# A chunked scan beside attention: the scan's steps divided anew

## The chip, the core and the metric

The kernel runs on one core of a Trainium2 chip. The metric is the device time in microseconds of one execution. The engines named below are TensorE (PE; its weight loads are PEld), VectorE (DVE), ScalarE (ACT), GpSimd (POOL) and SyncE (SP), whose queue issues most of the DMA transfers. All values are float32. A product marked 128*128 uses the whole array of TensorE, one marked 64*64 a quarter of it.

## The reference

One layer of a hybrid encoder for 1024 prompt tokens and 32 sample tokens that share the weights. `proj = x @ w_in` is split among three mixers: latent attention with 6 heads, a diagonal state space model (S5), and RWKV-7 time mixing with 6 heads of 64. Their outputs are concatenated, go through `w_out`, a layer norm, a squared-ReLU MLP of width 4096 and a second layer norm. The change lies in RWKV-7, whose recurrence for one head is

```python
def step(S, inp):
    r_t, w_t, k_t, v_t, kk_t, a_t = inp
    sa = jnp.einsum('bhij,bhj->bhi', S, -kk_t)
    S = (S * w_t[:, :, None, :] + sa[..., None] * (kk_t * a_t)[:, :, None, :]
         + v_t[..., None] * k_t[:, :, None, :])
    return S, jnp.einsum('bhij,bhj->bhi', S, r_t)
```

followed by a normalization of each head's output, a bonus term, a gate, and the final state as an output.

## The kernel before

The kernel has four parts in time: the input projections; attention and the scan side by side; the output projection with its layer norm; the MLP with the last layer norm.

The scan works on blocks of 128 tokens (two chunks of 64), nine of them in `ORDER` = (8, 0, 1, ..., 7), where block 8 holds the 32 sample tokens. Within a chunk the recurrence becomes products of 64 x 64 matrices, one for each of the 6 heads and 2 chunks. Heads go in three pairs: the two heads of a pair stand on partitions 0 to 63 and 64 to 127. So each product uses one quarter of TensorE's array, and which quarter follows from where its operands and its output lie. In `stage_rwkv` (L999) the pass i of the loop works on three blocks at once: t = ORDER[i] gets its chunk products and its solve, u = ORDER[i-1] gets its operators, its state steps and its mean, v = ORDER[i-2] is normalized and stored. The parts, with the names of their PSUM tiles:

- `rwkv_pairs` (t): pra, products masked by causality (L833, L835 on DVE); prt, four transposes for each of three head pairs (L840, copied by ACT in L841); prb (L846, L848); the weights of the bonus on POOL (L853, L854) and their sum prk (L856, L858).
- `rwkv_norm` (v): prv (L985), the inverse root on DVE and ACT, two POOL operations (L993, L994), a store to mg_d.
- `rwkv_ops` (u): prg, the transition and the readout (L897; L899 and L900 on DVE); pru, the sums U and Y (L906 to L912), a step for each head pair; then L917 (DVE) and L919 (ACT).
- `rwkv_nv` (t): prn (L868, L869). `rwkv_chain` (u): for each chunk pry (readout from the state, L940), prs (the new state, L944), L946 and L947 on DVE. `rwkv_mean` (u): prm (L968). `rwkv_solve` (t): prw with the inverse of the chunk's triangular matrix (L882, L883).

All of these tiles come from one PSUM pool, `g.pr`, with three slots; a tile waits until a slot has been released by its last reader.

What sets the order: all parts are generators, and each `yield` ends a step. `side_by_side` (L1299) takes steps from attention (with S5 among them) and from the scan in turn. After each scan step it lets RATIO attention steps pass (10 and 14 at the start). Every step's TensorE instructions are queued behind the last one of the step before (`issue_after`), so TensorE's order is the order of steps; within a step, and on the other engines, a scheduler orders at compile time by priority and estimated times, with the scan's steps 120 places ahead:

```python
while (n >= 1 or done[1]) and not done[0]:
    step(0, a)
    n -= 1
if not done[1]:
    ...
        step(1, b)
k += 1
n += LEAD[k] if k < len(LEAD) else RATIO
```

Every engine works through its own queue in order. When both streams are done, the output projection follows: `out_early` and `out_mm` for the first three token tiles, whose products the scheduler may place as soon as their operands are there, then `out_tile` (L1466) for the others, which loads its part of mg_d by L1431 and the residual z by L1478 in SP's queue. `out_weights` loads the eight tiles of `w_out` (L55, split in L49 and L50) into memory that the scan has given up: three at the end of pass 8, five after the loop.

Of the kernel before, what the change touches and what calls it, by code (L numbers as in the profile page):

```python
# [712 lines left out]
def hsl(i):  # L713
    return slice(64 * i, 64 * i + 64)
# [104 lines left out]
K_A, K_B, K_K, K_V, K_NV, K_N, K_KR, K_BR = range(8)  # L819


def rwkv_pairs(g, t):

    nc = g.nc
    mm = nc.tensor.matmul
    ld = g.ld[t]
    r = g.rp.tile([P, 3, 8, 2, 64], F32, tag="r", name="r", bufs=2)
    g.r[t] = r

    pa = [g.pr.tile([P, 3, 2, 64], F32, tag="pr", name="pra") for _ in range(2)]  # L830
    for p in range(3):
        for h, c in DIAG:
            mm(out=pa[h][hsl(c), p], lhsT=ld[hsl(h), p, 2, hsl(c)], rhs=ld[hsl(h), p, 0:5:4, hsl(c)], start=True, stop=True)  # L833
# [3 lines left out]
    for p in range(3):  # L837
        pt = g.pr.tile([P, 4, P], F32, tag="pr", name="prt")
        for i in range(4):
            nc.tensor.transpose(out=pt[:, i], in_=ld[:, p, i], identity=g.ident)  # L840
        nc.scalar.activation(out=r[:, p, 0:4].rearrange("q a h x -> q a (h x)"), in_=pt, func=AF.Copy)  # L841
        yield
    pb = [g.pr.tile([P, 3, 64], F32, tag="pr", name="prb") for _ in range(2)]
    for p in range(3):
        for h, c in DIAG:
            mm(out=pb[h][hsl(c), p], lhsT=ld[hsl(h), p, 1, hsl(c)], rhs=ld[hsl(h), p, 4, hsl(c)], start=True, stop=True)  # L846
    for h in range(2):
        nc.vector.tensor_tensor(out=r[:, :, K_BR, h], in0=pb[h], in1=bc(g.msk[:, 1:2], [P, 3, 64]), op=ALU.mult)  # L848
    yield

    w = blk_tokens(t)[1]
    x = r[:, :, K_NV].rearrange("q p h x -> q p (h x)")[:, :, :w]
    nc.gpsimd.tensor_tensor(out=x, in0=ld[:, :, 2, :w], in1=ld[:, :, 4, :w], op=ALU.mult)  # L853
    nc.gpsimd.tensor_tensor(out=x, in0=x, in1=bc(g.vec[:, V_RK:V_RK + 3][:, :, None], [P, 3, w]), op=ALU.mult)  # L854
    ps = g.pr.tile([P, 3, P], F32, tag="pr", name="prk")[:, :, :w]
    mm(out=ps, lhsT=g.bones, rhs=x, start=True, stop=True)  # L856
    g.bn[t] = g.rl.tile([P, 3, P], F32, tag="bn", name="bn", bufs=3)[:, :, :w]
    nc.vector.tensor_tensor(out=g.bn[t], in0=ps, in1=ld[:, :, 3, :w], op=ALU.mult)  # L858


def rwkv_nv(g, t):
# [7 lines left out]
    nc.scalar.activation(out=r[:, :, K_NV], in_=pn, func=AF.Copy)  # L869


def rwkv_solve(g, t):
    nc = g.nc
    r = g.r[t]
    wu = g.rp.tile([P, 3, 2, 2, 64], F32, tag="wu", name="wu", bufs=1)
    g.wu[t] = wu
    for p0, p1 in ((0, 2), (2, 3)):
        pw = g.pr.tile([P, p1 - p0, 2, 2, 64], F32, tag="pr", name="prw")
        for p in range(p0, p1):
            for h in range(2):  # L880
                for c in range(2):
                    nc.tensor.matmul(out=pw[hsl(c), p - p0, h], lhsT=g.xt[p][hsl(c), t, h], rhs=r[hsl(c), p, K_A:K_NV + 1:K_NV, h], start=True, stop=True)  # L882
        nc.scalar.activation(out=wu[:, p0:p1], in_=pw, func=AF.Copy)  # L883


def rwkv_ops(g, t):

    nc = g.nc
    mm = nc.tensor.matmul
    r, wu, ld = g.r.pop(t), g.wu.pop(t), g.ld.pop(t)  # L890
    gq = g.rl.tile([P, 2, 3, 3, 64], F32, tag="gq", name="gq", bufs=1)
    g.gq[t] = gq
    nch = 2 if t < 8 else 1
    pg = [g.pr.tile([P, 3, 2, 64], F32, tag="pr", name="prg") for _ in range(2)]
    for p in range(3):
        for c, h in DIAG:
            mm(out=pg[c][hsl(h), p], lhsT=wu[hsl(c), p, h, 0], rhs=r[hsl(c), p, K_B:K_BR + 1:K_BR - K_B, h], start=True, stop=True)  # L897
    for c in range(nch):
        nc.vector.tensor_tensor(out=gq[:, c, 0], in0=pg[c][:, :, 0], in1=bc(g.i2[:, None], [P, 3, 64]), op=ALU.add)  # L899
        nc.vector.tensor_tensor(out=gq[:, c, 1], in0=pg[c][:, :, 1], in1=ld[:, :, 4, hsl(c)], op=ALU.add)  # L900
    yield
    pu = [g.pr.tile([P, 3, 2, 64], F32, tag="pr", name="pru") for _ in range(2)]
    for p in range(3):
        for hc in (DIAG[0:2], DIAG[2:4]):
            for c, h in hc:
                mm(out=pu[c][hsl(h), p, 0], lhsT=r[hsl(c), p, K_B, h], rhs=wu[hsl(c), p, h, 1], start=True, stop=False)  # L906
            for c, h in hc:
                mm(out=pu[c][hsl(h), p, 0], lhsT=r[hsl(c), p, K_K, h], rhs=r[hsl(c), p, K_V, h], start=False, stop=True)
            for c, h in hc:
                mm(out=pu[c][hsl(h), p, 1], lhsT=wu[hsl(c), p, h, 1], rhs=r[hsl(c), p, K_BR, h], start=True, stop=False)  # L910
            for c, h in hc:
                mm(out=pu[c][hsl(h), p, 1], lhsT=r[hsl(c), p, K_V, h], rhs=r[hsl(c), p, K_KR, h], start=False, stop=True)  # L912
        yield
    yb = g.yb[t]
    for c in range(nch):
        k = 2 * t + c
        nc.vector.tensor_tensor(out=gq[:, c, 2], in0=pu[c][:, :, 0], in1=bc(g.pc[:, :, k:k + 1], [P, 3, 64]), op=ALU.mult)  # L917
        w = min(64, blk_tokens(t)[1])
        nc.scalar.activation(out=yb[:, :, 64 * c:64 * c + w], in_=pu[c][:, :, 1, :w], func=AF.Copy)  # L919


def rwkv_chain(g, t):

    nc = g.nc
    mm = nc.tensor.matmul
    gq = g.gq.pop(t)
    nch = 2 if t < 8 else 1
    py = g.pr.tile([P, 3, 2, 64], F32, tag="pr", name="pry")
    for c in range(nch):
        k = 2 * t + c  # L930
        if k in (0, 16):
            g.st = g.rl.tile([P, 3, 64], F32, tag="st", name="st", bufs=3)
            if k == 0:
                nc.gpsimd.memset(g.st, 0.0)
            else:
                nc.sync.dma_start(out=g.st, in_=g.a["s0"].rearrange("p j i -> j p i"))
        st = g.st
        for p in range(3):
            for h in range(2):
                mm(out=py[hsl(h), p, c], lhsT=st[hsl(h), p], rhs=gq[hsl(h), c, 1, p], start=True, stop=True)  # L940
        ps = g.pr.tile([P, 3, 64], F32, tag="pr", name="prs")
        for p in range(3):
            for h in range(2):
                mm(out=ps[hsl(h), p], lhsT=gq[hsl(h), c, 0, p], rhs=st[hsl(h), p], start=True, stop=True)  # L944
        sn = g.rl.tile([P, 3, 64], F32, tag="st", name="st", bufs=3)
        nc.vector.tensor_tensor(out=sn, in0=ps, in1=bc(g.pc[:, :, k:k + 1], [P, 3, 64]), op=ALU.mult)  # L946
        nc.vector.tensor_tensor(out=sn, in0=sn, in1=gq[:, c, 2], op=ALU.add)  # L947
        g.st = sn
        yield
        if k >= 15:  # L950
            pt = g.pr.tile([P, 3, P], F32, tag="pr", name="prq")
            for p in range(3):
                nc.tensor.transpose(out=pt[0:64, p], in_=sn[:, p], identity=g.ident)
            so = g.rl.tile([P, 3, P], F32, tag="m", name="so", bufs=1)[0:64]
            nc.scalar.activation(out=so, in_=pt[0:64], func=AF.Copy)
            nc.scalar.dma_start(out=g.o["rw_p" if k == 15 else "rw_s"].rearrange("h i j -> i h j"), in_=so.rearrange("i p (h j) -> i (p h) j", h=2))
    w = blk_tokens(t)[1]
    ys = g.yb[t][:, :, :w]
    nc.vector.tensor_tensor(out=ys, in0=ys, in1=py[:, :, 0:nch].rearrange("q p c x -> q p (c x)")[:, :, :w], op=ALU.add)


def rwkv_mean(g, t):
# [36 lines left out]
def stage_rwkv(g):  # L999
# [9 lines left out]
    for p in range(3):  # L1009
# [7 lines left out]
            nc.sync.dma_start(out=x[0:32, 0:16, 32:64], in_=src[c][2][:, 0:16])  # L1017
        g.xt[p] = xt

    for i in range(10):  # L1020
        t, u, v = (ORDER[j] if 0 <= j < 9 else None for j in (i, i - 1, i - 2))
        if i + 2 < 9:
            rwkv_load(g, ORDER[i + 2])
        if t is not None:
            yield from rwkv_pairs(g, t)
        if v is not None:
            rwkv_norm(g, v)
            yield
        if u is not None:
            g.yb[u] = g.rl.tile([P, 3, P], F32, tag="yb", name="yb", bufs=2)  # L1030
            yield from rwkv_ops(g, u)
        if t is not None:
            rwkv_nv(g, t)
            yield
            if u is not None:
                yield from rwkv_chain(g, u)
                rwkv_mean(g, u)
            rwkv_solve(g, t)
            yield
        if i == 8:  # L1040
            out_weights(g, WOUT[:3])
    out_weights(g, WOUT[3:])


def stage_rwkv_end(g):
    yield from rwkv_chain(g, ORDER[8])
    rwkv_mean(g, ORDER[8])
    rwkv_norm(g, ORDER[8])


# [10 lines left out]
    yield from stage_rwkv_end(g)  # L1061


RATIO, LEAD, PRIO = 2.5, (10, 14), 120
S5_FROM, S5_STEP = 50, 7


# [803 lines left out]
```

## Time and profile before

| | us |
|---|---|
| median of 3 runs | 1610.53 (1609.14 to 1616.11) |
| the profiled execution | 1609.9 |
| its span, first to last instruction | 1608.1 |
| TensorE busy | 1487.7 (93%) |
| VectorE busy | 920.6 (57%) |
| ScalarE busy | 510.6 (32%) |
| GpSimd busy | 415.9 (26%) |

The first product of the scan's first block (pra) starts at 366.24 us, the last products of attention (av) at 722.69, the last of the scan (prv) at 744.77. In the rows, a timeline line has start, length, engine, line of the code, operation, output<-inputs, shape and count; in brackets stands how long the engine was idle before and what ended that.

### The profile page before, as it was taken

How to read it: one execution, taken by the hardware profiler on the slowest of the kernel's cores; microseconds unless marked ns; L12 is line 12 of the kernel's file. 1: busy time of each engine (PE TensorE's matmuls, PEld its weight loads, DVE VectorE, ACT ScalarE, POOL GpSimd, SP SyncE). 2: the span in 40 equal slices, each digit the busy share in tenths (PEclk: the TensorE clock that was granted, in tenths of full speed). 3: DMA queues.
4: the chain of work that ended last, by engine and by line, in shares of the span. 5: the costliest groups of instructions: out<-in, count | busy, mean ns of one | idle time of the engine just before them, and what ended most of it. 6: DMA issues, size and time to landing. Idle time of an engine off the chain costs nothing. (4 is left out here: it accounts for less than half of the span.)

```text
span 1608.1 us, 26358 instructions
## 1 busy us (share of the span) xinstructions
PE 1487.7 (93%) x10855; PEld 1336.1 (83%) x10855; DVE 920.6 (57%) x1676; ACT 510.6 (32%) x991; POOL 415.9 (26%) x394
## 2 busy tenths in 40 slices
PE   7899898578899798888999999999999999999995
PEld 7889786466667566566879999999999999999995
DVE  8476959363566544453865755554454454545457
ACT  5344433314544545542323212222121112221122
POOL 4623663511121101211422221222121112221123
PEclk9999999788999999999999999999999999999998
DMA  5314471437233221233512111111111111111012
GB/s 183 132 59 175 148 191 31 115 87 127 71 86 87 63 75 42 72 98 92 174 56 79 40 40 41 52 53 49 44 43 50 40 40 53 53 40 53 14 41 82
DMA packets 112621, 123.50 MB, mean 77 GB/s; under 512 B 51280, under 2 KB 87812, under 8 KB 112120
## 3 DMA queue, kind: packets, MB, share of 16 engines
q1 hardware_dynamic: 92516, 102.53, 21.8%
q10 hardware_dynamic: 19632, 18.27, 3.8%
q8 instruction: 85, 1.39, 0.4%
q0 software_dynamic: 352, 1.01, 0.2%
q14 instruction: 36, 0.29, 0.1%
HBM read 89.05 MB, written 32.68 MB: 76 GB/s over the span
## 5 line engine op out<-in xcount | busy, mean ns | idle before, releaser
L63 PE MATMUL acc<-xh,uphi 128*128 128x384 f32 (+1 forms) x768 | 249.0, 324 | 0.0
L65 PE MATMUL acc<-xl,uphi 128*128 128x384 f32 (+1 forms) x768 | 248.1, 323 | 0.0
L67 PE MATMUL acc<-xh,uplo 128*128 128x384 f32 (+1 forms) x768 | 247.8, 323 | 0.0
L1538 DVE TENSOR_TENSOR rl<-rl 128x384 f32<-128x384 f32 (+1 forms) x96 | 142.2, 1481 | 176.2 <-ACT rl L1537 174.3
L1566 DVE TENSOR_TENSOR yacc<-yacc,acc 128x384 f32<-128x384 f32 (+2 forms) x344 | 158.9, 508 | 112.1 <-PE acc L67 112.0
L63 PE MATMUL acc<-hh,dnhi 128*128 128x384 f32 (+2 forms) x736 | 209.3, 320 | 0.0
L65 PE MATMUL acc<-hl,dnhi 128*128 128x384 f32 (+2 forms) x736 | 207.2, 320 | 0.0
L67 PE MATMUL acc<-hh,dnlo 128*128 128x384 f32 (+2 forms) x736 | 197.5, 319 | 0.0
L50 POOL TENSOR_TENSOR dnlo<-dnraw,dnhi 128x1024 fp32r<-128x1024 f32 x30 | 72.5, 2417 | 336.8 <-ACT dnhi L49 321.5
L63 PEld LDWEIGHTS acc<-xh,uphi 128*128 128x128 f32 x768 | 144.2, 188 | 0.2 <-ACT xh L49 0.2
L65 PEld LDWEIGHTS acc<-xl,uphi 128*128 128x128 f32 x768 | 144.3, 188 | 0.0
L67 PEld LDWEIGHTS acc<-xh,uplo 128*128 128x128 f32 x768 | 144.3, 188 | 0.0
L50 POOL TENSOR_TENSOR uplo<-upraw,uphi 128x1024 fp32r<-128x1024 f32 x34 | 81.6, 2401 | 238.3 <-ACT uphi L49 238.3
L63 PE MATMUL acc<-xh,wmhi 128*128 128x384 f32 (+3 forms) x384 | 131.9, 344 | 9.3 <-ACT xh L49 8.2
L65 PE MATMUL acc<-xl,wmhi 128*128 128x384 f32 (+3 forms) x384 | 130.2, 339 | 1.6 <-DVE xl L50 1.6
L63 PEld LDWEIGHTS acc<-hh,dnhi 128*128 128x128 f32 x736 | 131.6, 188 | 0.0
L65 PEld LDWEIGHTS acc<-hl,dnhi 128*128 128x128 f32 x736 | 131.5, 188 | 0.0
L67 PE MATMUL acc<-xh,wmlo 128*128 128x384 f32 (+3 forms) x384 | 129.6, 338 | 0.0
L67 PEld LDWEIGHTS acc<-hh,dnlo 128*128 128x128 f32 x736 | 128.9, 188 | 0.0
L49 ACT ACTIVATE dnhi<-dnraw 128x1024 fp32r<-128x1024 f32 x30 | 31.8, 1060 | 298.9 <-PE acc L65 249.2
L49 ACT ACTIVATE hh<-rl 128x384 fp32r<-128x384 f32 (+1 forms) x96 | 47.9, 499 | 148.7 <-DVE rl L1538 148.7
L63 PEld LDWEIGHTS acc<-xh,wmhi 128*128 128x128 f32 (+1 forms) x384 | 73.9, 192 | 12.8 <-ACT xh L49 8.5
(489 smaller groups left out, 2881.2 us busy)
## 6 DMA issues: line engine op xcount, KB each, us to landing
upraw<-in_w_up SPq DMA_DIRECT2D x32, 512.0 KB
dnraw<-in_w_dn SPq DMA_DIRECT2D x30, 512.0 KB
ld<-rw SPq DMA_DIRECT2D x24, 320.0 KB
wmraw<-in_w_m SPq DMA_DIRECT2D x12, 512.0 KB
wo<-in_w_out SPq DMA_DIRECT2D x8, 512.0 KB
z<-in_xa SPq DMA_DIRECT2D x8, 512.0 KB
out_y<-o SPq DMA_DIRECT2D x8, 512.0 KB
xr<-in_xt SPq DMA_DIRECT2D x8, 384.0 KB
```

Of the source, the lines that this page charges most:

```text
L49: nc.scalar.activation(out=hi, in_=ps, func=AF.Copy)
L50: (lo_eng or nc.vector).tensor_tensor(out=lo, in0=ps, in1=hi.bitcast(F32), op=ALU.subtract)
L63: nc.tensor.matmul(out=outs[i], lhsT=lh, rhs=rhs[i][0], start=start, stop=False)
L65: nc.tensor.matmul(out=outs[i], lhsT=lh, rhs=rhs[i][1], start=False, stop=False)
L67: nc.tensor.matmul(out=outs[i], lhsT=ll, rhs=rhs[i][0], start=False, stop=stop)
L1538: nc.vector.tensor_tensor(out=r[:, :n], in0=r[:, :n], in1=r[:, :n], op=ALU.mult)
L1566: nc.vector.tensor_tensor(out=y, in0=y, in1=ps[i][:, :n], op=ALU.add)
```

## The change

The arithmetic stays the same. The scan's functions are cut so that each can be called by itself, and the loop puts them into other steps. `rwkv_pairs` becomes `rwkv_causal`, `rwkv_turn` (one head pair), `rwkv_br`, `rwkv_weigh` (the POOL part of the bonus) and `rwkv_bonus`; `rwkv_ops` becomes `rwkv_gq` and `rwkv_uy`; `rwkv_solve` takes a range of head pairs; `rwkv_chain` does one chunk, with the products for the new state ahead of those for the readout; the transposes of the final states are `rwkv_state`. A full pass has 9 steps instead of 14:

| before | after |
|---|---|
| pra | pra |
| prt of pair 0 | prt of pairs 0 and 1 |
| prt of pair 1 | weights of the bonus, prt of pair 2, prm of v |
| prt of pair 2 | prb |
| prb | prk, normalization of v |
| prk, normalization of v | prg, prn |
| prg | pru of all three pairs, U and Y evicted |
| pru of pair 0 | state step of chunk 0, prw of pairs 0 and 1 |
| pru of pair 1 | state step of chunk 1, prw of pair 2 |
| pru of pair 2 | |
| U and Y evicted, prn | |
| state step of chunk 0 | |
| state step of chunk 1 | |
| end of the chain, prm of u, prw | |

The mean of a block (prm) so moves from its own pass into the next. The last block's state steps move into the loop, ahead of the loads of the last five output weights. RATIO goes from 2.5 to 3.6.

```diff
     for i in range(10):
         t, u, v = (ORDER[j] if 0 <= j < 9 else None for j in (i, i - 1, i - 2))
         if i + 2 < 9:
             rwkv_load(g, ORDER[i + 2])
         if t is not None:
-            yield from rwkv_pairs(g, t)
+            rwkv_causal(g, t)
+            yield
+            rwkv_turn(g, t, 0)
+            rwkv_turn(g, t, 1)
+            yield
+            x = rwkv_weigh(g, t)
+            rwkv_turn(g, t, 2)
+        if v is not None:
+            rwkv_mean(g, v)
+            if v == 8:
+                rwkv_state(g, 16)
+        yield
+        if t is not None:
+            rwkv_br(g, t)
+            yield
+            rwkv_bonus(g, t, x)
         if v is not None:
             rwkv_norm(g, v)
-            yield
+        yield
         if u is not None:
             g.yb[u] = g.rl.tile([P, 3, P], F32, tag="yb", name="yb", bufs=2)
-            yield from rwkv_ops(g, u)
+            rwkv_gq(g, u)
         if t is not None:
             rwkv_nv(g, t)
+        yield
+        if u is not None:
+            rwkv_uy(g, u)
             yield
-            if u is not None:
-                yield from rwkv_chain(g, u)
-                rwkv_mean(g, u)
-            rwkv_solve(g, t)
-            yield
+            rwkv_chain(g, u, 0)
+        if t is not None:
+            rwkv_solve(g, t, 0, 2)
+        yield
+        if u is not None and chunks(u) > 1:
+            rwkv_chain(g, u, 1)
+        if t is not None:
+            rwkv_solve(g, t, 2, 3)
+        yield
         if i == 8:
             out_weights(g, WOUT[:3])
     out_weights(g, WOUT[3:])
...
 def stage_rwkv_end(g):
-    yield from rwkv_chain(g, ORDER[8])
     rwkv_mean(g, ORDER[8])
+    rwkv_state(g, 15)
+    yield
     rwkv_norm(g, ORDER[8])
...
-def rwkv_chain(g, t):
+def rwkv_chain(g, t, c):
...
+    gq = g.gq[t]
+    if c == 0:
+        g.py = g.pr.tile([P, 3, 2, 64], F32, tag="pr", name="pry")
+    k = 2 * t + c
...
+    st = g.st
+    ps = g.pr.tile([P, 3, 64], F32, tag="pr", name="prs")
+    for p in range(3):
+        for h in range(2):
+            mm(out=ps[hsl(h), p], lhsT=gq[hsl(h), c, 0, p], rhs=st[hsl(h), p], start=True, stop=True)
+    for p in range(3):
+        for h in range(2):
+            mm(out=g.py[hsl(h), p, c], lhsT=st[hsl(h), p], rhs=gq[hsl(h), c, 1, p], start=True, stop=True)
...
-def rwkv_ops(g, t):
+def rwkv_uy(g, t):
...
     pu = [g.pr.tile([P, 3, 2, 64], F32, tag="pr", name="pru") for _ in range(2)]
     for p in range(3):
         for hc in (DIAG[0:2], DIAG[2:4]):
...
-        yield
...
-RATIO, LEAD, PRIO = 2.5, (10, 14), 120
+RATIO, LEAD, PRIO = 3.6, (10, 14), 120
```

More of the change, by code (lines that the diff above doesn't have):

```diff
@@ L819, with rwkv_causal @@
 K_A, K_B, K_K, K_V, K_NV, K_N, K_KR, K_BR = range(8)
[L822 removed]
+def rwkv_causal(g, t):
     nc = g.nc
[L825 removed]
     ld = g.ld[t]
@@ L869, in rwkv_nv, with rwkv_solve, chunks, rwkv_gq @@
     nc.scalar.activation(out=r[:, :, K_NV], in_=pn, func=AF.Copy)
-def rwkv_solve(g, t):
+def rwkv_solve(g, t, p0, p1):
     nc = g.nc
     r = g.r[t]
[L875 to L883, printed above, removed]
-def rwkv_ops(g, t):
+    if p0 == 0:
+        g.wu[t] = g.rp.tile([P, 3, 2, 2, 64], F32, tag="wu", name="wu", bufs=1)
+    pw = g.pr.tile([P, p1 - p0, 2, 2, 64], F32, tag="pr", name="prw")
+    for p in range(p0, p1):
+        for h in range(2):
+            for c in range(2):
+                nc.tensor.matmul(out=pw[hsl(c), p - p0, h], lhsT=g.xt[p][hsl(c), t, h], rhs=r[hsl(c), p, K_A:K_NV + 1:K_NV, h], start=True, stop=True)
+    nc.scalar.activation(out=g.wu[t][:, p0:p1], in_=pw, func=AF.Copy)
+def chunks(t):
+    return 2 if t < 8 else 1
+def rwkv_gq(g, t):
     nc = g.nc
-    mm = nc.tensor.matmul
-    r, wu, ld = g.r.pop(t), g.wu.pop(t), g.ld.pop(t)
+    r, wu, ld = g.r[t], g.wu[t], g.ld.pop(t)
     gq = g.rl.tile([P, 2, 3, 3, 64], F32, tag="gq", name="gq", bufs=1)
     g.gq[t] = gq
-    nch = 2 if t < 8 else 1
     pg = [g.pr.tile([P, 3, 2, 64], F32, tag="pr", name="prg") for _ in range(2)]
@@ L912, in rwkv_ops @@
                 mm(out=pu[c][hsl(h), p, 1], lhsT=r[hsl(c), p, K_V, h], rhs=r[hsl(c), p, K_KR, h], start=False, stop=True)
-        yield
     yb = g.yb[t]
-    for c in range(nch):
+    for c in range(chunks(t)):
         k = 2 * t + c
@@ L919, in rwkv_ops @@
         nc.scalar.activation(out=yb[:, :, 64 * c:64 * c + w], in_=pu[c][:, :, 1, :w], func=AF.Copy)
-def rwkv_chain(g, t):
+def rwkv_chain(g, t, c):
     nc = g.nc
     mm = nc.tensor.matmul
[L926 to L959, printed above, removed]
@@ new lines, in rwkv_chain @@
+    for p in range(3):
+        for h in range(2):
+            mm(out=g.py[hsl(h), p, c], lhsT=st[hsl(h), p], rhs=gq[hsl(h), c, 1, p], start=True, stop=True)
+    sn = g.rl.tile([P, 3, 64], F32, tag="st", name="st", bufs=3)
+    nc.vector.tensor_tensor(out=sn, in0=ps, in1=bc(g.pc[:, :, k:k + 1], [P, 3, 64]), op=ALU.mult)
+    nc.vector.tensor_tensor(out=sn, in0=sn, in1=gq[:, c, 2], op=ALU.add)
+    g.st = sn
+    if c == chunks(t) - 1:
+        w = blk_tokens(t)[1]
+        ys = g.yb[t][:, :, :w]
+        nc.vector.tensor_tensor(out=ys, in0=ys, in1=g.py[:, :, 0:c + 1].rearrange("q p c x -> q p (c x)")[:, :, :w], op=ALU.add)
+        g.gq.pop(t)
@@ L962, in rwkv_mean, with rwkv_state @@
+def rwkv_state(g, k):
+    nc = g.nc
+    pt = g.pr.tile([P, 3, P], F32, tag="pr", name="prq")
+    for p in range(3):
+        nc.tensor.transpose(out=pt[0:64, p], in_=g.st[:, p], identity=g.ident)
+    so = g.rl.tile([P, 3, P], F32, tag="m", name="so", bufs=1)[0:64]
+    nc.scalar.activation(out=so, in_=pt[0:64], func=AF.Copy)
+    nc.scalar.dma_start(out=g.o["rw_p" if k == 15 else "rw_s"].rearrange("h i j -> i h j"), in_=so.rearrange("i p (h j) -> i (p h) j", h=2))
 def rwkv_mean(g, t):
```

54 lines of the change are left out of this document (36 added, 18 removed).

## The prediction

> **What bounds the kernel now.** I read the engine shares and the 40 slices first, then busy time by stage, then who waits for whom on TensorE in the stage that the change touches, and last the order of instructions there. The chain of waits on the page covers only the last few instructions, so it is not used.
>
> ```profile
> PE 1487.7 (93%) x10855; PEld 1336.1 (83%) x10855; DVE 920.6 (57%) x1676; ACT 510.6 (32%) x991; POOL 415.9 (26%) x394
> PE   7899898578899798888999999999999999999995
> ```
>
> TensorE is busy 93% of the span, and from slice 20 on it is full: what is gained before about 780 us is kept to the end. The stages (stretch, length, busy us of PE, PEld, DVE, ACT, POOL, then granted clock and DMA):
>
> ```profile
> 366.00:706.00 340.00, 303.86 (x3207) 225.08 (x3207) 180.96 (x408) 166.97 (x357) 51.25 (x111) 0.95 0.30 75
> 706.00:752.00 46.00, 44.56 (x324) 33.74 (x325) 21.69 (x37) 16.32 (x27) 4.72 (x8) 1.00 0.29 86
> 752.00:780.00 28.00, 21.76 (x88) 17.24 (x87) 17.34 (x28) 8.44 (x22) 14.09 (x10) 0.88 0.69 221
> 780.00:830.00 50.00, 49.83 (x240) 39.90 (x239) 34.47 (x60) 11.81 (x33) 10.21 (x13) 1.00 0.29 85
> ```
>
> The scan and the attention run side by side in the first of these. TensorE works 303.86 of 340 us (89%); no other engine passes 181. So the stage is TensorE's work plus 36 us in which its in-order queue stands. Who ended the longest of these waits (us in total, times, longest):
>
> ```profile
> PE av L1255 <- POOL ptk L1282: 9.2, 6, 4.2
> PE pra L833 <- DMA ld<-rw: 6.7, 2, 6.5
> PE sck L1119 <- DVE kl L50: 4.9, 3, 2.6
> PE prb L846 <- ACT r L841: 3.8, 1, 3.8
> PE pry L940 <- DVE st L947: 2.6, 4, 1.4
> ```
>
> Only pry, prb and pra belong to the scan; the others are attention's own.
>
> **One block of the scan.** The order of TensorE's work in one undisturbed block (quarter-array products have 64*64, full ones 128*128):
>
> ```profile
> 534.28 1.15 PE L833 MATMUL pra<-ld 64*64 64x128 f32 x24
> ...
> 558.75 0.33 PE L906 MATMUL pru<-wu,r 64*64 64x64 f32 x2
> ...
> 559.04 0.27 PE L906 MATMUL pru<-wu,r 64*64 64x64 f32 x1
> ...
> 559.50 0.27 PE L906 MATMUL pru<-wu,r 64*64 64x64 f32 x1
> ...
> 560.10 0.33 PE L63 MATMUL st<-qh,kh 128*128 128x128 f32 x1
> ...
> 561.98 0.33 PE L906 MATMUL pru<-wu,r 64*64 64x64 f32 x4
> ...
> 562.27 0.27 PE L906 MATMUL pru<-wu,r 64*64 64x64 f32 x2
> ...
> 562.88 0.50 PE L63 MATMUL sc<-kh,qh 128*128 128x512 f32 x1
> ...
> 564.33 0.33 PE L906 MATMUL pru<-wu,r 64*64 64x64 f32 x4
> ...
> 565.23 0.28 PE L63 MATMUL st<-qh,kh 128*128 128x32 f32 x1
> ...
> 566.05 0.92 PE L868 MATMUL prn<-r 64*64 64x64 f32 x24
> 569.25 0.57 PE L940 MATMUL pry<-gq,st 64*64 64x64 f32 x12
> 571.02 0.56 PE L940 MATMUL pry<-gq,st 64*64 64x64 f32 x12 [0.19 <-DVE st L947]
> 573.51 1.53 PE L882 MATMUL prw<-r,xt 64*64 64x128 f32 x24
> 576.12 1.16 PE L833 MATMUL pra<-ld 64*64 64x128 f32 x24
> ```
>
> A block takes 576.12 - 534.28 = 41.8 us and visits the quarter arrays ten times (pra, prb, prg, pru three times, prn, pry twice, prw). The change leaves six. What a visit costs beside its work can be read at one of the state steps:
>
> ```profile
> 610.12 0.28 PE L65 MATMUL sc<-kl,qh 128*128 128x128 f32 x1
> 610.23 0.27 PE L67 MATMUL sc<-kh,ql 128*128 128x128 f32 x1
> 610.44 0.56 PE L940 MATMUL pry<-gq,st 64*64 64x64 f32 x12
> 610.84 0.52 PE L944 MATMUL prs<-st,gq 64*64 64x64 f32 x12
> 611.28 0.38 PE L63 MATMUL sc<-kh,qh 128*128 128x256 f32 x1
> ```
>
> A full product of 128 columns takes a turn of 0.11 us (610.12 to 610.23), so the first quarter product, at 610.44, comes 0.10 late. The 24 records on two quarters start over 0.70 us (12 turns of 0.06); the last starts at about 611.14, and the next full product 0.14 later, 0.08 more than a turn. A visit costs 0.18 us.
>
> **The change part by part.**
>
> (a) The three visits of L906 to L912 become one. Now they take 560.10 - 558.75 = 1.35, 562.88 - 561.98 = 0.90 and 565.23 - 564.33 = 0.90, together 3.15 us from first product to next full one. The second and third show how one head pair flows: two halves, one on each diagonal of the array, the second starting 0.29 us after the first (561.98, 562.27) while the first still runs. Six halves in a row take 5 x 0.29 + (0.90 - 0.29) = 2.06. That is 1.09 less, and two entries of 0.10 less: 1.29 us a block, 11.6 in nine. The other bound: in the first visit the four groups start one after another on single quarters (558.75, 559.04, ..., 559.50: 0.25 apart), as if the sum pru of the second chunk had no PSUM slot yet when the order was fixed. If all three pairs are issued so, twelve groups take 11 x 0.25 + 0.60 = 3.35: 0.20 more, and with the two entries saved nothing is won. I take the first, because two visits of three flow so and because the slots have 3.6 attention steps to come free, not 2.5; both ends are kept.
>
> (b) prn joins prg, and the two state steps and prw become two visits out of three: two visits less, 0.36 us a block, about 3.1 in eight and a half. No overlap is counted; at most it could add that of prn's 0.92 with prg.
>
> (c) The two state steps stand 3.6 attention steps apart. An attention step lasts about 0.77 us: the rows of the block leave some 27 of the 41.8 us to 35 steps. So the cover of the update (L946, L947) grows from 1.9 to 2.8 us, and of the 2.6 us that pry waits I take 2 as gone. The products for the new state also stand ahead of those for the readout.
>
> (d) Ahead of the first pra there are 1.1 attention steps more: 0.85 us of its 6.5 us wait for ld. The loads themselves are not moved.
>
> (e) Moved, and counted as nothing: the weights for the bonus (POOL) two steps ahead of their product, covered by TensorE's own queue; the mean of a block into the next block, behind the third turn, where its one product of L968 waits for nothing that is late; three transposes, a copy and a store for the final states. If the cover for the mean were gone, its 0.56 us on DVE would stand ahead of the normalization, which no product waits for before the last block:
>
> ```profile
> 739.47 0.56 DVE L970 SCALAR_TENSOR_TENSOR yc<-prm,yb 128x384 f32<-128x384 f32 x1 [5.58 <-PE prm L968]
> ```
>
> (f) The end. By the counts of the two generators attention and S5 have 343 steps; they end with three of the scan's 132 steps left, and with five of its 95 after the change. So the last block's U/Y products fall behind the end of attention, and the loads and splits of five of the eight output weights are issued behind the last two state steps rather than ahead of them. There the scan's end is what the next stage waits for:
>
> ```profile
> 755.83 0.94 SPq L1431 DMA_DIRECT2D mraw<-mg_d  x2
> ...
> 762.99 0.77 PE L63 MATMUL acc<-wo,mh 128*128 128x512 f32 x1 [6.24 <-DVE z L1488]
> ```
>
> SP's queue stands until the last block is stored, z is behind it, and TensorE idles 6.24 us. The U/Y products move both the end of TensorE's fill-in work and the scan's end by their own 2 us, so the gap stays; a later split of a weight or a copy that stands in line can widen it by up to the 4.5 us shown below, under R3. The low end is minus 2 (with fewer splits ahead of the state updates). I take 1.5.
>
> Sum: 11.6 + 3.1 + 2 + 0.85 = 17.5 us of TensorE's time. Not all of it arrives. The five rows of waits above alone are 16 stops, one in 21 us, and most end on another engine's chain; what is saved in the last 6 us or so before such a stop, when that chain is already running, only lengthens it. The 6 us are a guess of two or three steps on each side. That makes three tenths, so 12.3 are left; less 1.5 at the end, 10.8. From the profiled execution's 1609.9 that gives 1599. The median of the runs is 1610.53, 0.6 above, and doesn't move the forecast.
>
> **The rivals.**
>
> R1, the four quarters are not filled: the U/Y products go group by group as in the first visit above. Then 5.9 us are saved, 4.1 arrive, and 1607 is the time. For it: every block's first visit goes so today. Against it: the longer gap ahead of it.
>
> R2, the saving comes back as waits: attention's chains (mx, kl, ptk) set the pace, and TensorE only stands longer. Time 1610. For it: 36 us of waiting already; against: DVE is at 53% of the stage and TensorE at 89%.
>
> R3, slower: PSUM. The pool has three slots. Today the widest steps want two new ones; now prg with prn wants three, the first state step with its solve wants three, and each must wait, with all of attention behind it in TensorE's in-order queue, until DVE and ACT have emptied the ones before.
>
> ```profile
> L917 DVE TENSOR_TENSOR gq<-pru,pc 128x192 f32<-128x192 f32 x17 | 5.3, 353 | 10.8 <-PE pru L912 10.6
> L919 ACT ACTIVATE yb<-pru 128x192 f32<-128x192 f32 x16 | 4.7, 326 | 10.1 <-DVE gq L917 10.1
> ...
> 710.28 0.89 PE L897 MATMUL prg<-r,wu 64*64 64x128 f32 x24
> 714.89 0.35 DVE L900 TENSOR_TENSOR gq<-prg,ld 128x192 f32<-128x192 f32 x1
> 720.79 0.28 PE L912 MATMUL pru<-r 64*64 64x64 f32 x4
> 725.08 0.53 ACT L919 ACTIVATE yb<-pru 128x192 f32<-128x192 f32 x2
> ```
>
> At best the four evictions of pru take 2 x 0.35 + 2 x 0.33 = 1.4 us, inside the 2.8 us of cover. In the stretch from 710 on, where other work stood in line, prg was empty 715.24 - 711.17 = 4.1 us after its products and pru 725.61 - 721.07 = 4.5. If every block went so, 1.3 + 1.7 = 3 us a block would be lost, 27 in nine: 1626. It decides, against 10.8 gained, once the evictions take about 4 us on the mean. Against it: DVE and ACT mostly stood idle before these two rows (10.8 and 10.1 us), so the short value is the nearer one. The Trainium skill warns of this very thing ("TensorEngine Tiling (Array Packing)", section PSUM Bottleneck): tiling speeds up TensorE, not the copies out of PSUM, which can then become the bound; in this trace the copies keep up except at the end.
>
> **How the numbers follow.** Forecast 0.50 (1599, its own range 1591 to 1604), R1 0.22 (1607), R2 0.15 (1610), R3 0.13 (1626 at full price, 1618 at two thirds). About 0.5%, 8 us, is what a measurement of this kernel can tell from no change. Faster than that, below 1602.5: 0.85 of the forecast's share and a fifth to a quarter of R1's, 0.48. Slower, above 1618.6: R3 and a fifth of R2, 0.16. The rest, 0.36, is within. The range 1588 to 1617 takes in both ends of (a) and of (f) and the lower part of R3; it leaves out R3 at full price and a saving that arrives whole with prg and prn overlapped.
>
> **What would show it.** Six visits of the quarter arrays a block in TensorE's order, not ten. L906 to L912 as one visit: about 2.1 us if (a) is right, 3.3 if R1 is. pry's wait for L947 near nothing. PE busy between the first pra and the end of attention lower by 15 to 18 us if the gain is in the work; if it is lower by that and the stretch is no shorter, R2. A new wait of prn, prs or prw on L900, L917 or L919 is R3. The gap before the fourth output tile should stay at 5 to 9 us. The forecast is wrong if the stretch from the first pra to the last av shrinks by less than 6 us.

## The result and the profile after

The changed kernel takes 1629.42 us (median of 4 runs, 1627.45 to 1631.46), the kernel before 1610.55 beside it: ratio 1.0104, 95% interval 1.0071 to 1.0137. It is 17 to 19 us slower. The profiled execution took 1628.62 us. The forecast was 1599 with a range to 1617; it was wrong in sign. Two executions among the experiments, the profiled one of a1_s5_later (7440 us) and one of b3_before_s5_later (8010 us), were disturbed and stand outside all figures, so that a1 has no rows below.

The engines' shares and TensorE's 40 slices of the changed kernel (columns as before):

```profile
PE 1481.3 (91%) x10855; PEld 1334.5 (82%) x10855; DVE 921.6 (57%) x1676; ACT 510.8 (31%) x991; POOL 416.3 (26%) x394
PE   7899897677898778889899999999999999999995
```

TensorE is busy 6.4 us less in all (1487.7 before), with as many instructions, and the last half of the slices is as full as before: the time was lost between slices 9 and 20. Here is that stretch, from the first product of the scan (pra) to the gap before the fourth output tile, in each kernel (stretch, length, busy us of PE with count, of PEld, DVE, ACT, POOL, then TensorE's granted clock, DMA share, GB/s). Before:

```profile
366.24:756.75 390.51, 353.16 (x3550) 262.30 (x3550) 202.65 (x445) 183.29 (x383) 57.56 (x120) 0.96 0.30 76
```

After:

```profile
364.35:775.41 411.06, 350.33 (x3534) 264.41 (x3534) 202.03 (x441) 182.30 (x380) 57.50 (x118) 0.89 0.30 72
```

The stretch grew by 20.6 us. The prediction's own sign, the stretch from the first pra to the last av, was to shrink by 6 us or more; it grew from 356.45 us (366.24 to 722.69) to 376.80:

```profile
741.15 0.38 PE L1307 MATMUL av<-ptk,vo 128*128 128x128 f32 x2
```

For the longer stretch above, length less busy time is what TensorE stood: 37.4 us before, 60.7 after. It worked 2.8 us less, though at 0.89 of its clock in place of 0.96. Who ended its waits there, in the changed kernel (us in total, times, longest):

```profile
PE prw L899 <- ACT wu L900: 10.1, 1, 10.1
PE s5e L633 <- DMA em<-em_d: 7.7, 1, 7.7
PE pra L832 <- DMA ld<-rw: 7.4, 1, 7.4
PE av L1307 <- POOL ptk L1334: 5.8, 6, 2.4
PE av L1307 <- ACT ptk L1332: 5.6, 1, 5.6
...
PE prw L899 <- ACT yb L943: 1.4, 1, 1.4
PE pra L832 <- DVE st L969: 1.2, 1, 1.2
```

The first two and the fifth are new; each is a single long stop. pry's wait for the state is gone; what is left of it is 1.2 us, once, at pra.

**The stop at S5's first product.** The queue of SP ahead of it (start, length, queue, line, transfer):

```profile
371.82 0.50 SPq L1045 DMA_DIRECT2D xt<-xt_d  x1
372.42 2.93 SPq L814 DMA_DIRECT2D ld<-rw  x3
375.40 0.52 SPq L619 DMA_DIRECT2D ut<-u_d  x1
375.97 0.67 SPq L620 DMA_DIRECT2D ut<-u_d  x1
376.68 0.72 SPq L622 DMA_DIRECT2D em<-em_d  x1
```

and TensorE's row for it:

```profile
381.73 1.23 PE L633 MATMUL s5e<-ut,em 128*128 128x133 f32 x4 [7.70 <-DMA em<-em_d]
```

SP issues S5's loads last, behind 18 loads of xt and 9 of ld. It did so before as well. There, TensorE started the product without a wait:

```profile
377.85 1.73 SPq L622 DMA_DIRECT2D em<-em_d  x1
...
383.25 0.69 PE L633 MATMUL s5e<-ut,em 128*128 128x133 f32 x4
```

That is 17.0 us after the first pra (366.24). Now TensorE is there 9.7 us after it (374.03 against 364.35). The cause is in the steps: S5's first step stands at attention step 56 in both kernels, the first pra at step 39 before and 45 after. The scan's stream has seven short steps ahead of pra. The first two follow 10 and 14 attention steps, 24 in all, and after that six gaps of RATIO steps lie ahead of pra: 24 + 6 x 3.6 = 45.6 in place of 24 + 6 x 2.5 = 39.

The stop costs more than its length. Windows of the changed kernel behind it, and behind the stop at L899:

```profile
381.70:383.00 1.30, 1.27 (x5) 1.30 (x6) 0.00 (x0) 0.00 (x1) 0.00 (x0) 0.50 0.15 44
...
387.00:389.00 2.00, 2.00 (x6) 1.17 (x4) 0.77 (x5) 0.60 (x1) 0.00 (x0) 0.50 0.00 0
...
390.00:391.00 1.00, 1.00 (x5) 0.20 (x3) 0.00 (x0) 0.00 (x0) 0.00 (x0) 0.56 0.00 0
391.00:392.00 1.00, 1.00 (x26) 0.93 (x26) 0.68 (x1) 0.01 (x1) 0.00 (x0) 1.00 0.00 0
601.88:603.00 1.12, 1.12 (x9) 0.79 (x9) 0.00 (x0) 0.43 (x1) 0.00 (x0) 0.50 0.00 0
...
605.00:606.00 1.00, 1.00 (x3) 0.34 (x1) 0.00 (x0) 0.21 (x1) 0.00 (x0) 0.54 0.06 16
606.00:607.00 1.00, 1.00 (x6) 0.83 (x5) 0.07 (x1) 0.00 (x0) 0.00 (x0) 1.00 0.00 0
```

After the 7.70 us TensorE runs at half its clock from 381.7 to about 390.8: 9 us, in which, by an estimate of half of it, 4.5 us of work are lost. After the 10.05 us it is 4 us. The Trainium skill ("TensorE: Matmul & The Clock Gate", Part 1) states half rate until about 3.4 us of sustained work. The 4 us behind the second stop are near that figure; the 9 us behind the first are more than twice as long.

**The stop at the solve.** ScalarE's queue:

```profile
586.79 0.23 ACT L1316 ACTIVATE rec<-rec 64x32 f32<-64x32 f32 x1
596.65 1.28 ACT L683 ACT_TABLE_LOAD   x1 [9.63 <-DMA zt<-z_d]
597.94 1.98 ACT L683 ACTIVATE zt<-zt 128x2128 f32<-128x2128 f32 x1
599.93 1.28 ACT L76 ACT_TABLE_LOAD   x1
601.23 0.60 ACT L900 ACTIVATE wu<-prw 128x512 f32<-128x512 f32 x1
```

S5's GELU stands 9.63 us for its 16 loads, and the copy of prw stands behind it, with TensorE behind the copy. In the kernel before, the same GELU stood less, and held up a copy of prt (the 3.8 us of prb in the prediction's waits):

```profile
584.76 1.28 ACT L683 ACT_TABLE_LOAD   x1 [3.35 <-DMA zt<-z_d]
```

The third new stop (av on ptk, 5.6 us) comes from the split of an early output piece: ScalarE's queue stands at it until the piece is loaded.

**What the change does inside a block.** TensorE's order has six visits of the quarter arrays. The joined product, in the block at 539:

```profile
539.32 0.33 PE L931 MATMUL pru<-wu,r 64*64 64x64 f32 x4
...
541.19 0.28 PE L937 MATMUL pru<-r 64*64 64x64 f32 x4
541.40 0.28 PE L1285 MATMUL scm<-ident,m 128*9 128x128 f32 x1
```

It takes 541.40 - 539.32 = 2.08 us. The gap before the fourth output tile is nearly as it was:

```profile
782.23 0.77 PE L63 MATMUL acc<-wo,mh 128*128 128x512 f32 x1 [6.82 <-DVE z L1540]
```

### The profile page after: what moved, and what is told of

The parts are those of the page before. It is cut to its first block, busy times and chain, and to the rows that moved or that the text cites. A ratio compares the mean times of both kernels' runs of the same rounds, so it can differ in the third digit from the quotient of the medians.

```text
span 1626.8 us, 26364 instructions
## 1 busy us (share of the span) xinstructions
PE 1481.3 (91%) x10855; PEld 1334.5 (82%) x10855; DVE 921.6 (57%) x1676; ACT 510.8 (31%) x991; POOL 416.3 (26%) x394
## 5 line engine op out<-in xcount | busy, mean ns | idle before, releaser
L1307 PE MATMUL av<-ptk,vo 128*128 128x512 f32 (+5 forms) x204 | 76.9, 461 | 14.3 <-POOL ptk L1334 5.8
```

Source lines behind the costliest of these rows:

```text
L1307: nc.tensor.matmul(out=po[:, c:n], lhsT=vo[:w, kt].rearrange("p a x -> p (a x)")[:, 64 * i:64 * i + P], rhs=pt[:w, c:n], start=kt == tiles ...
```

## The experiments

**Theories.** T: the work is saved as forecast, and what is lost is lost at a few places, where an engine's in-order queue has come to stand before a transfer, because the new RATIO shifts every attention and S5 step against the scan's. W (the prediction's R2, beyond parity): fewer, larger scan steps leave attention's own waits uncovered, so the saving comes back wherever it is made. In the expectations, steps a block are the stream's whole count (132 before, 95 after, 113 with pru apart) over nine blocks. All ratios are against the kernel before on the same chip. The groups of runs came from different chips, so where two kernels of different groups are compared, the ratios are the safer figure.

**1. The three stops, one at a time and together.** `a1_s5_later`:

```diff
-S5_FROM, S5_STEP = 50, 7
+S5_FROM, S5_STEP = 57, 7
```

> The changed kernel with S5_FROM 57 instead of 50: S5's first step, whose product waited 7.70 us for the load of em, comes seven attention steps later. Theory T (the joined steps save about 9 us of TensorE's work, but attention and S5 reach some places sooner than a DMA round trip that an in-order queue stands before; three of them make most of the new 30 us of waiting): the wait for em goes, with the slow clock behind it, 1618 to 1622 us. Rival W (the wide steps with their three PSUM sums at once set the pace, and a wait that is taken away comes back elsewhere): 1627 to 1631.

1615.1 us, ratio 1.0014 (0.9994 to 1.0034): some 14 us come back by this edit alone, more than T said.

`a2_gelu_later` emits the GELU two S5 steps later:

```diff
-    log_exp_table(g, [... AF.Gelu_apprx_tanh ...], False)
     yield
     yield
+    log_exp_table(g, [... AF.Gelu_apprx_tanh ...], False)
+    yield
```

> The changed kernel with S5's GELU two of S5's steps (14 attention steps) behind the loads of its input instead of at once: on ScalarE's in-order queue it no longer stands before a DMA that has not landed (9.63 us there; TensorE stood 10.05 us behind it for a copy out of PSUM). T: TensorE's wait of prw for that copy goes, 1614 to 1621 us. W: the solve's copy waits for a slot all the same, 1626 to 1631.

1630.3 us, 1.0121 (1.0084 to 1.0158): nothing. TensorE's row shows why:

```profile
604.45 0.91 PE L900 MATMUL prw<-r,xt 64*64 64x128 f32 x6 [9.90 <-ACT wu L901]
```

The wait is the same, since the scheduler put the GELU between the same neighbours on ScalarE. Only an order that is demanded moves it, as in experiment 3; a2 says nothing for or against T.

`a3_split_later` (the split of the early output rows' piece with k = 2 issued behind the attention's last ScalarE instruction):

```diff
-        split3(g, raw, hi, lo, g.nc.gpsimd)
+        with g.tc.issue_after(g.mix_act) if k == 2 else nullcontext():
+            split3(g, raw, hi, lo, g.nc.gpsimd)
```

> The changed kernel with one early split of the output projection (the part of heads 4 and 5) queued on ScalarE behind attention's last instruction: it waited 7.16 us there for its load, and TensorE 5.64 us for the exponentials behind it. T: 1620 to 1626 us. W: 1627 to 1631.

1627.14 us, 1.0101 (1.0065 to 1.0137). The wait of 5.6 us fell to 2.1, and a new one stood next to it:

```profile
PE acc L63 <- ACT wo L49: 4.3, 1, 4.3
PE av L1307 <- ACT ptk L1332: 2.1, 1, 2.1
```

`a4_all_three` has all three edits:

> All three edits in the changed kernel: S5 seven attention steps later, GELU two of its steps behind its loads, the split of heads 4 and 5 behind attention. T: 7.7 + 10 + 5.6 us of waits and some 5 us of slow clock go, 1597 to 1606 us, faster than the kernel before. W: 1618 us or more.

1620.12 us, 1.0052 (1.0034 to 1.0071): a miss for T, and slower than a1 alone. The GELU now stood one copy later, and TensorE waited 10.16 us at the next thing behind it:

```profile
592.12 1.22 PE L1308 MATMUL av<-ptk,vo 128*128 128x512 f32 x1 [10.16 <-ACT ptk L1333]
```

**2. Is it SP's queue?** `b1_s5_loads_act` leaves all steps where the change has them:

```diff
-        nc.sync.dma_start(out=u[:, :, 0:P], in_=src[:, :, 0:P])
-        nc.sync.dma_start(out=u[:, :, P + 1:NY], in_=src[:, :, P:NC5])
+        dma = nc.sync if q else nc.scalar
+        dma.dma_start(out=u[:, :, 0:P], in_=src[:, :, 0:P])
+        dma.dma_start(out=u[:, :, P + 1:NY], in_=src[:, :, P:NC5])
...
-        nc.sync.dma_start(out=em, in_=g.em_d[:, gs])
+        dma.dma_start(out=em, in_=g.em_d[:, gs])
```

> After's kernel, S5 steps where they were; only the first S5 group's three loads (two of u, one of em) are issued on ScalarE's queue in place of SyncE's, where they stood behind 18 loads of xt and 9 of ld and were issued at 375.40 to 376.68 us. Theory T (what is late is the load, held back in SyncE's queue): TensorE's wait of 7.70 us for em is under 2 us and the time is 1613 to 1621 us. Rival W (the larger steps cover the attention's waits badly all along): the wait goes, another comes within 40 us of it, and the time stays at 1625 to 1631 us. Rival D (the loads are slow because the DMA engines are shared, not because of the queue): the wait stays at 4 us or more, or the wait of 7.39 us for ld before it grows by as much.

1617.09 us, 1.0034 (1.0014 to 1.0053). The load goes out at 360.57 instead of 376.68:

```profile
360.57 0.53 ACTq L623 DMA_DIRECT2D em<-em_d  x1
```

and the windows that held the stop and the half clock are full and fast:

```profile
374.00:381.70 7.70, 7.70 (x70) 6.13 (x69) 4.57 (x13) 4.59 (x14) 0.00 (x0) 1.00 0.92 153
381.70:389.00 7.30, 7.30 (x64) 5.11 (x63) 2.79 (x5) 4.04 (x9) 0.30 (x2) 1.00 0.47 115
```

pra's wait for ld stayed (7.28 us, 7.4 before the edit), so D falls. From 1.0104 to 1.0034 is 0.70%, 11.3 us, near 7.70 plus the 4.5 of half clock. This stop is the largest part of the loss, and the place in the queue is its cause.

**3. S5 later and the GELU really later.** `b2_s5_gelu` is a1 with

```diff
-    log_exp_table(g, [... AF.Gelu_apprx_tanh ...], False)
+    yield
+    yield
+    yield
+    yield
+    with g.tc.issue_after(last_traced(g, mybir.EngineType.Activation)):
+        log_exp_table(g, [... AF.Gelu_apprx_tanh ...], False)
     yield
-    yield
```

> S5's first step 7 attention steps later (S5_FROM 57) as before, and the GELU issued on ScalarE after the ScalarE instruction of four S5 steps later, so that it stands some 28 rows further back on that engine, behind the copies of prw and prt that it held up. Theory T: the 10.05 us in which TensorE waited for ScalarE's copy at 591.83 us go too; with the S5 load's wait gone the time is 1602 to 1609 us. Rival W: the wait is taken over by another place (S5's own later steps, or the attention's keys) and the time stays at 1613 to 1618 us, where the S5 change alone put it (1615.1).

1612.03 us, 0.9986 (0.9969 to 1.0003). The 10 us wait is gone; the kernel is level with before, not 10 us ahead. T's range (1602 to 1609) is missed, and so is W's (1613 to 1618), by little. Against a1 it is 3 us by the medians and 4.5 by the ratios, whose intervals overlap. `b3_before_s5_later` is the control, the kernel before with S5_FROM 57:

> The kernel before with the same S5_FROM 57. Its S5 steps had no wait of this kind (1.01 us in all for em). Theory T (S5's first loads collided because the new ratio brought the scan's first step later beside them): no gain, 1607 to 1617 us. Rival G (a later S5 is better in any kernel of this form, so that it says nothing of the change): 1602 us or less.

1615.37 us, 1.0008 (0.9987 to 1.0029): no gain, so a1's gain belongs to the new step order.

**4. The rest of the places.** `c1_three_waits` is b2 with the loads of b1 and with a3's edit from the fourth piece on (`if j >= 3`):

> The kernel of b2_s5_gelu with the first S5 group's loads on ScalarE's queue besides, and the splits of the last three pieces of the early output rows (from the fourth piece on) issued on ScalarE behind the attention's last ScalarE instruction. In b2's trace TensorE waited 1.90 us for em at 384.06 and 6.00 us for ScalarE at 689.57, where ScalarE stood 9.26 us at such a split. Theory T (what is lost is lost at such places, one by one): both waits go, 1603 to 1608 us. Rival W (TensorE's saved time comes back as waits wherever they are): the waits come up elsewhere and the time stays within 3 us of 1612.

1611.71 us, 0.9998 (0.9982 to 1.0014). Both waits went. In their place, among others, av waits for ScalarE's po and prs for the state:

```profile
PE av L1312 <- ACT po L1317: 6.5, 2, 3.6
...
PE prs L969 <- DVE st L975: 4.9, 2, 2.5
```

Here W's forecast holds: what is taken away at this size comes up elsewhere. At the other RATIO of experiment 6 it is less plain: there the same two edits (c4 to d3) go with 2.5 us by the medians and 5.6 by the ratios, with intervals that overlap. `c3_before_gelu_split` gives the kernel before the same care (GELU and late splits):

> The kernel before with the same two edits on ScalarE's order: the GELU four S5 steps later behind a ScalarE instruction of that place, and the late pieces' splits behind the attention's last ScalarE instruction. Before's trace has 3.78 us of TensorE's wait at the GELU and 4.25 us at such a split. Theory T (the places are what costs, in both kernels): 1603 to 1609 us, so that the new division does not lead at equal care. Rival L (before is free of such waits to within what can be measured): 1609 to 1615 us.

1606.57 us, 0.9958 (0.9939 to 0.9976): the old division had 7 us of such stops to give.

**5. The join undone.** `c2_product_apart` is b2 with

```diff
                 mm(out=pu[c][hsl(h), p, 1], lhsT=r[hsl(c), p, K_V, h], ...)
+        if p < 2:
+            yield
...
-            rwkv_uy(g, u)
+            yield from rwkv_uy(g, u)
...
-RATIO, LEAD, PRIO = 3.6, (10, 14), 120
+RATIO, LEAD, PRIO = 3.03, (10, 14), 120
```

> The kernel of b2_s5_gelu with the change's largest part undone: the twelve kinds of the product pru stand in three steps, one head pair each, as before; 12.55 steps a block in place of 10.55, and 3.03 attention steps for one of the scan in place of 3.6 (both 38.0 a block). The work is the same. Theory T (a visit saved is time saved where TensorE sets the end): TensorE's busy time from the first scan product to the output tile grows by 8 to 13 us against b2's 342.8 and the time by as much: 1619 to 1625 us. Rival W (TensorE does not set the end here; its saved time became waits): busy time grows by as much, the waits shrink by as much, and the time stays within 4 us of 1612.

1605.45 us, 0.997 (0.9951 to 0.999): with the change's largest saving taken out the kernel is no slower than b2, and by the medians 6.6 us faster (2.6 by the ratios). The stretch from the first pra to the output tile, in b2:

```profile
368.74:760.33 391.59, 342.75 (x3534) 258.03 (x3534) 202.83 (x441) 181.85 (x380) 57.28 (x118) 0.91 0.31 77
```

and in c2:

```profile
367.37:751.93 384.56, 350.09 (x3542) 266.05 (x3542) 200.43 (x443) 182.52 (x384) 57.38 (x120) 0.93 0.32 79
```

TensorE worked 7.3 us more with pru apart, and stood 34.5 us in place of 48.8. Neither range is met: T's time is missed by 14 us, and the waits shrank by twice what W said. Waits that shrank the most, in b2:

```profile
PE av L1311 <- POOL ptk L1338: 10.6, 9, 2.9
PE av L1311 <- ACT ptk L1336: 8.5, 2, 6.0
...
PE sck L1175 <- DVE ml L50: 5.8, 2, 3.7
```

in c2, where the last is not in the list any more:

```profile
PE av L1313 <- POOL ptk L1340: 6.7, 6, 2.4
...
PE av L1313 <- ACT ptk L1338: 1.0, 1, 1.0
```

These are attention's own products. Most are behind other engines' chains, but the 6.0 us in b2 are one stop at a split of an early output piece, for which ScalarE stood 9.26 us; so part of the 14.4 us is where one instruction fell. To tell the join from luck, two more pairs follow. `d1_only_product_apart` is the changed kernel with this edit alone:

> The changed kernel with nothing altered but pru in three steps again (12.55 steps a block) and 3.03 in place of 3.6, so that a block still takes 38.0 attention steps; S5's loads and the GELU are where the change had them. Theory J (the join pays TensorE 7 to 10 us but returns more in waits): 1612 to 1622 us. Theory Q (the loads' places cost all of it; the join pays): 1630 to 1640 us. Nothing between them: 1623 to 1629 us, the join is worth nothing either way.

1624.99 us, 1.0079 (1.0054 to 1.0105): neither J nor Q, the join is worth nothing either way. Its stretch:

```profile
366.11:768.53 402.42, 351.80 (x3542) 265.73 (x3542) 200.69 (x443) 182.14 (x382) 56.80 (x119) 0.92 0.30 74
```

`c4_gelu_ratio_347` and `d2_apart_ratio_292` are b2 and c2 at another RATIO (3.47 and 2.92; below):

> The kernel of b2_s5_gelu with 3.47 in place of 3.6 attention steps for one of the scan. Theory T: no wait of more than 5 us is made or removed by it but where an instruction happens to fall; 1606 to 1616 us. Rival P (the scan is stretched over too many attention steps): under 1605 us, since 3.47 alone took 5 us off after's kernel.

> c2's kernel (S5 later, GELU later, pru in three steps) at the pace of c4: 2.92 x 12.55 = 36.6 attention steps a block. c4, the same with pru joined, took 1602.3 us. Theory J (the join costs in waits): 1595 to 1600 us. Theory Q (the join saves 7 to 10 us of TensorE's time and c2's lead over b2 was a matter of places): 1606 to 1613 us. Neither: 1600 to 1606.

1602.29 us, 0.9949 (0.9929 to 0.997), joined, and 1601.0 us, 0.9919 (0.9888 to 0.995), apart, which is neither J nor Q again. Their stretches, joined (c4):

```profile
364.99:748.48 383.49, 339.24 (x3537) 255.61 (x3537) 201.78 (x442) 183.10 (x381) 57.63 (x118) 0.94 0.33 81
```

and apart (d2):

```profile
363.17:747.12 383.95, 348.73 (x3544) 260.17 (x3544) 203.04 (x443) 184.64 (x383) 57.01 (x120) 0.94 0.33 83
```

At one granted clock the join saves 9.5 us of TensorE's time (the other two pairs: 7.3, and 1.5 where the clock was 0.89 against 0.92), and TensorE stands 9.0 us longer (14.4; 10.1). In time, joined against apart is +4.4, +6.6 and +1.3 us in the three pairs by the medians, +4.0, +2.6 and +4.8 by the ratios: each within the intervals, none a gain. The pairs differ in RATIO too, so that a block keeps its number of attention steps; they show the join together with the wider spacing that goes with it, not one without the other.

**6. The pace.** `b4_ratio_347` is the changed kernel with RATIO 3.47 and nothing else:

> After's kernel with 3.47 attention steps for one of the scan in place of 3.6, so that nine blocks take as many attention steps as before (10.55 x 3.47 = 36.6; before 14.67 x 2.5 = 36.7). Theory T: the first scan product comes 0.8 attention steps earlier against S5's first step, the wait for em falls by a us or so, the GELU falls on another place; 1616 to 1629 us. Rival P (after is slow because the scan is stretched over too many attention steps): 1608 to 1614 us. Rival W: 1626 to 1634 us.

1624.2 us, 1.007 (1.0045 to 1.0096). `d4_before_pace` is c3 with 2.41 in place of 2.5, `d3_joined_all_edits` c4 with the remaining edits of c1:

> c3's kernel (before, with GELU and late splits moved) at 2.41 in place of 2.5 attention steps for one of the scan (the same 3.6% as from 3.6 to 3.47). It shows how far the pace alone moves the old division: by what places alone do, 1600 to 1613 us; if a denser scan is better in any division, as c4 was 10 us faster than b2, under 1600 us.

> c4's kernel with the S5 group's loads on ScalarE's queue and the late splits behind the attention's last ScalarE instruction. c4's trace has TensorE's wait for em of 2.13 us and 3.68 us for ScalarE at 705.03. Both theories: 1597 to 1603 us, if these two waits go and nothing comes in their place; if waits only change their place, 1602 to 1608 us.

d4: 1597.79 us, 0.9914 (0.9886 to 0.9943). d3: 1599.82 us, 0.9914 (0.9891 to 0.9938). Both beat both kernels.

| attention steps beside the scan's stream | old division | pru apart | joined |
|---|---|---|---|
| 342, S5 and GELU moved | | 1605.5 | 1612.0, 1611.7 |
| 330, S5 and GELU moved | 1606.6 (GELU, splits) | 1601.0 | 1602.3, 1599.8 |
| 318, GELU and splits moved | 1597.8 | | |
| 342, no edit | | 1625.0 | 1629.4 |
| 330, no edit | 1610.6 (before) | | 1624.2 |

A denser scan is faster in each of the five pairs that differ in it alone (after and b4 5 us, b2 and c4 10, c2 and d2 4, c3 and d4 9, c1 and d3 12). The intervals of the first four just touch or overlap; those of c1 (0.9982 to 1.0014) and d3 (0.9891 to 0.9938) stand clear of each other. What it shortens is seen in b2 and c4. The last av and the fourth output tile in b2:

```profile
724.26 0.38 PE L1311 MATMUL av<-ptk,vo 128*128 128x128 f32 x2
...
766.81 0.76 PE L63 MATMUL acc<-wo,mh 128*128 128x512 f32 x1 [6.49 <-DVE z L1544]
```

and in c4:

```profile
724.12 0.38 PE L1311 MATMUL av<-ptk,vo 128*128 128x128 f32 x2
...
753.40 0.77 PE L63 MATMUL acc<-wo,mh 128*128 128x512 f32 x1 [4.92 <-DVE z L1544]
```

Attention ends at the same time; what follows it, with the scan's end in it, is 13.3 us shorter. The prediction's own count of steps fits this. With 343 attention steps, 3.6 leaves five of the 95 scan steps behind the end of attention and 3.47 leaves two; with pru apart, 3.03 leaves six of 113 and 2.92 two; in the old division 2.5 leaves three of 132 and 2.41 none. From the last av to the fourth output tile the time falls in every pair: from 41.08 to 24.81 us (after, b4), 42.55 to 29.28 (b2, c4), 45.13 to 27.45 (c1, d3), 43.42 to 35.20 (c2, d2) and 39.56 to 23.25 (c3, d4). Not all of it arrives: in b4 and d4 attention itself ends later, at 757.06 in place of 741.15 and at 729.03 in place of 719.21.

## Why the prediction was wrong

**(a) was sized right.** One joined visit takes 2.08 us where 2.06 was worked out; R1 (3.35) falls. Joined against apart at equal clock is 9.5 us of TensorE's time (c4, d2) where (a) had 11.6. With (b), c4's busy time is 353.16 - 339.24 = 13.9 us below before's, at 0.94 of the clock against 0.96; (a) and (b) had 14.7. The work was saved.

**The step that failed first is the one from the sum to the time**: "three tenths" lost to the stops that follow. That share was a guess, and the runs show the whole of (a) lost: none of the three pairs gains time, and TensorE stood 9.0 to 14.4 us longer in each joined kernel. R2, given 0.15, is what happened to the saving. The prediction read TensorE's 89% as the bound and let the 36 us of waits grow by three tenths of the saving only. They grew by nearly all that the join saves: 9.0 us for 9.5 in c4 and d2. Attention's chains run through ACT, DVE and POOL, and the scan's visits are what TensorE does meanwhile. That two visits fewer leave more of these waits uncovered fits the waits of b2 and c2 in part, but is argued, not shown: no run changed the cover alone. The list of waits was also misread: pra's 6.5 us end at 366.24, so that all but 0.24 of them lie ahead of the 340 us stage and are no part of its 36 us.

**The second is (d) and (e), and it made level into slower.** (d) said 1.1 attention steps more ahead of the first pra; it is six scan steps with 1.1 each, 6.6 in all. (d) also said that the loads are not moved. They are not, but TensorE's arrival at S5's first product moved towards them: 17.0 us behind the first pra became 9.7. That cost 7.70 us and the half clock behind them, 11 to 14 us by b1 and a1. (e) listed what the diff moves and left out what RATIO moves: every attention and S5 step against the scan, the GELU of 9.63 us among them. In SP's queue the prediction had the scan's loads in view only. And the ld wait itself did not shrink by 0.85 us: it is 7.4. In both kernels SP issues ld right behind the stores of the scan's last short step, at 359.18 us before and 357.70 after, and TensorE comes to pra at 359.75 and 356.97. So the steps that RATIO puts ahead of pra stand ahead of the load as well, and cover none of it.

**The pace was not in the sum.** The scan's stream stands beside 132 x 2.5 = 330 attention steps before and 95 x 3.6 = 342 after (the longer lead of its first two steps not counted). 3.47 keeps it at 330 and is 5 us faster (b4). As attention has 343 steps, 342 leave the scan's last steps to run alone, as experiment 6 shows.

**Together.** S5's load (11 to 14 us), the pace (5), the GELU (about 3) and the 8.1 us of (a) that were to arrive (seven tenths of 11.6) make 27 to 30 of the 30 us between forecast and result. That is an estimate: the pieces come from different kernels, and a1 to a4 show that they do not simply add.

**(c)** held in the changed kernel: pry's wait is gone. With S5 and the GELU moved, a wait for the same state is back at prs, the first product of the state step now (2.6 us in b2, 4.9 in c1). **(f)** held: the gap is 6.82 us (6.24 before), and from the last av to the fourth output tile it is 41.08 us (40.30 before), where 1.5 us more were forecast. **R3** did not come: its sign, prw's wait for the copy of pru (L943, L919 before), appears once with 1.4 us; the 10.1 us of prw on L900 carry one of R3's names but are the GELU's.

TensorE's busy time from the first pra to the end of attention was to be lower by 15 to 18 us. It is lower by 2.9 in the changed kernel (316.5 against 319.5), with the clock at 0.88 against 0.95.

**What stays open**: why the saved time came back as waits, and whether the new division is worth anything at equal care. At 330 steps it is 1602.3 or 1599.8 against 1606.6, but the edits are not the same in both, and the old one reaches 1597.8 at 318.

## What to carry to other kernels

When two streams are interleaved by a ratio, count what the new ratio does to every step of both: find each place where a queue waits for a transfer, and ask how many us of the other stream now stand ahead of it. Where one engine is 89% busy and the rest is waits on chains through others, work saved on it is not yet time; joining small steps may also take away what covered those waits. Count too how many steps of one stream are left when the other ends. Before judging a new division, move the few large stops and the ratio in the old one too: that gave 0.9% here, as much as in the new one.

## What was not expected of the hardware

A stop of 7.70 us was followed by 9 us at half the granted clock, one of 10.05 us by only 4. And an instruction that is emitted two steps later need not be issued later: ScalarE's order around the GELU, and TensorE's wait of 9.90 us, stayed as they were (a2).
